# A gate's sums of squares by column blocks, and two token tiles to a PSUM bank

## The chip, the cores and the metric

The program runs on one core of a Trainium2 chip. The time is the device time of one execution in microseconds (us); a kernel's time is the median of its runs. The profile comes from one more execution of the same program.

## What is computed

Two layers of an encoder trunk on 512 tokens of 1024 values, all in float32. Each layer has mixers (three groups of heads), a layer of 16 experts that each take 64 tokens, and at its end an embedding that is let in through a gate. The change is in this last part:

```
x = x + expert_choice_ffn(rmsnorm(x, g_ffn), ...)          # 16 experts; the last two matter here
e = rmsnorm(p[i] @ w_ple, g_ple)                           # computed earlier
gate = sigmoid(rmsnorm(x, g_ple_gate) @ w_ple_gate)        # [512, 1024] @ [1024, 1024]
x = x + e * gate
```

where `rmsnorm(x, g) = x * rsqrt(mean(x * x) + eps) * g`, the mean over a token's 1024 values.

## The kernel before

The 512 tokens are four token tiles of 128 (index t), the 1024 columns four column blocks of 256 (index c) or eight row blocks of 128 (index k) where they are contracted. A product in full float32 quality is made of three single-pass matmuls (`mm3`, lines 340 to 342): both operands are kept as a high and a low part, and the product of the two low parts is left out.

The function `moe` ends as follows. The last two experts' down projection goes by column blocks. For each c, TensorE multiplies with weights `wd` (line 1385) into `pY`; ScalarE and VectorE split the result into `yh` and `yl` (lines 1387, 1388); TensorE scatters them to the tokens, one product pair per token tile (lines 1392, 1393, PSUM tile `ysc`); VectorE adds that to x (line 1395). With that the columns of block c of x are final. TensorE then transposes them (line 1400, `nt`), and ScalarE and VectorE split the transposed block into `gTh` and `gTl` (the helper `split`, lines 269 and 271): the left operand of the gate's product, two row blocks k for each c. The norm is not applied to this operand: its gain g_ple_gate goes with the weights' rows, and its factor is applied when the product is read.

After the four blocks come four squares on ScalarE, one for each token tile, over all 1024 columns, each with an accumulated sum (line 1410). From the four sums VectorE makes the norm's factor `rg` by the helper `rsqrt`: four preparing steps (lines 175 to 178) and three Newton steps of three instructions (180 to 182), all on [128, 4], and a halving (1413).

Then the gate's products. For each column block c of the weights, and each token tile t, TensorE runs 8 x 3 matmuls into a PSUM tile `pgp` of [128, 256] (lines 340 to 342); ScalarE takes the tanh with `rg` as its scale (line 1425), VectorE does two steps with the embedding (1426) and x (1428), and in the last layer SyncE stores the block (1430). In layer 0 all of x is stored to a scratch (1434), for the next layer to read.

The PSUM tiles `pgp` and `pY` come from a pool of four buffers of one bank (2 KB per partition) each (`pg`). A buffer is given again when all who used it are done: for `pgp`, when the tanh has read it. The [128, 256] tile takes one such buffer and half of its bytes.

The gate's weights are loaded by SyncE's queue in four column blocks, multiplied by the gain on GpSimd (line 329), and split into `whi` on ScalarE (330) and `wlo` on GpSimd (332), each in four pieces of two row blocks. These and other large arrays take turns in 12 slots of 8 KB.

Semaphores and the order of the instructions on each engine are made by a planner, which simulates the program with its own costs and lets an engine take what is ready first, in the order of the text where several are. So gate products of block 0 stand between the last down projections in TensorE's order. The order on each engine is then fixed.

Of the kernel before, what the change touches and what calls it, by code (L numbers as in the profile page):

```python
# [15 lines left out]
ALU = mybir.AluOpType  # L16
# [20 lines left out]
# the tensor engine's waits in a step of the scan, in us  # L37
OWED = 0.5
# the pieces that go ahead of the scan
INIT = 3  # L40
FILLS = (1.9, 1.5, 1.1)
# the convolved columns' blocks of 128 (q 0-2, k 3-5, v 6-8) by column tiles, and w_out's tiles for groups A and B
# [4 lines left out]
def shape_constants():  # L47
    """Arrays that depend on the shapes alone, in one [128, n] block."""
# [36 lines left out]
    # log of the number of patterns that join two tokens, by partition and column offset  # L85
# [10 lines left out]
# per-layer small parameters by partition: [128, DEPTH, n]  # L96
PP = {"conv": (0, 45), "b_s": (45, 4), "qk_g": (49, 2), "g_ffn": (51, 8), "g_pg": (59, 8)}
PPW = 67
# per-layer row parameters, the same for every partition: [DEPTH, n]
# [5 lines left out]
def rr_(ap):  # L105
    """the same bytes, as operands of the single-pass product"""
    return ap.bitcast(F32R)


class K:  # L110
# [25 lines left out]
    def slot(self, name):  # L136
        """one of the 8 KB buffers that weights and passing activations share"""
        return self.cp.tile([128, 2048], F32, tag="slot", name=name, bufs=SLOTS)

    def gslot(self, name):  # L140
        """the same, for the scan's own arrays"""
        return self.cp.tile([128, 2048], F32, tag="gslot", name=name, bufs=2)

    def half(self, name):
        """half of such a buffer"""
        if self.halves is None:
            tv = self.slot(name)
            self.halves = tv[:, 1024:]
            r = tv[:, 0:1024]
        else:  # L150
            r, self.halves = self.halves, None
        return r.rearrange("p (k n) -> p k n", k=4)
# [16 lines left out]
    # ---- small helpers  # L169
    def rsqrt(self, y, ss, n, scale, eps):  # L170
        """y = (ss * scale + eps) ** -0.5 by three Newton steps; y, ss [128, n]; returns ss * scale + eps"""
# [13 lines left out]
    def rsqrt1(self, y, ss, scale, eps):  # L185
        """the same for one column"""
# [11 lines left out]
    # ---- start  # L198
# [12 lines left out]
    def setup2(self, l):  # L211
        """what only the mixers need"""
        nc, A = self.nc, self.A
        if l == 0:
            nc.scalar.dma_start(self.pp, A["pp"])
        self.mconst = self.one([128, CROUTE - CKEEP], "mcst")
        nc.scalar.dma_start(self.mconst, A["cst"][:, CKEEP:CROUTE])
        self.amask = self.one([128, S + 384], "amask")
# [39 lines left out]
    # ---- RMS norm of one token tile, with its gain  # L258
# [8 lines left out]
    def split(self, hi, lo, src, scale=1.0):  # L267
        """src (in PSUM) * scale as the sum of two parts that the single-pass product carries exactly"""
# [6 lines left out]
    def norm_T(self, t, h, hi, lo):  # L275
        """h [128 tokens, D] transposed into columns t of hi and lo, each a pair of [128, 4, S]"""
# [8 lines left out]
    # ---- weights  # L285
    def wtile(self, src, cols, nk=KD):
        """src [nk*128, cols] dram view, rows k*128+p -> [128, nk, cols]"""
# [4 lines left out]
    def wplan(self, specs):  # L292
        """(src, cols, nk) of the pairs that wnext will hand out, in their order"""
# [3 lines left out]
    def wload(self, small=False):  # L297
        """starts the load of the next weights, into one buffer or four small ones"""
# [12 lines left out]
    def wnext(self, ahead=True, small=False, gain=None, pieces=1, dve=0):  # L311
        """the next weights, times a gain by rows, as two parts that the single-pass product carries exactly"""
# [24 lines left out]
    def mm3(self, p, lh, ll, rh, rl, first, last):  # L337
        """p += (lh + ll).T @ (rh + rl) without the product of the two small parts"""
# [5 lines left out]
    def proj_tok(self, w, t, name):  # L344
        """token tile t of xn times the column tiles w"""
# [9 lines left out]
    def proj_cols(self, p, w, t, ks, k0=0):  # L355
        """the rows ks of one of these products, w from row k0"""
# [5 lines left out]
    # ---- one layer's mixers  # L362
    def mixer(self, l):
        nc, tc, A = self.nc, self.tc, self.A
        with tc.tile_pool(name=f"mix{l}", bufs=1, reuse_waits="tile") as mp:
# [5 lines left out]
            # in the order in which they end  # L371
# [32 lines left out]
            # the chunks' matrices wait for q and k alone  # L404
# [13 lines left out]
            # the scan's steps, and between them what does not wait for it  # L418
# [8 lines left out]
    def in_order(self):  # L427
        """a function that traces a generator's next piece, for the tensor engine after the pieces before it"""
# [17 lines left out]
    def interleave(self, lead, fill):  # L446
        """traces lead, whose pieces end with the time that the tensor engine would then wait, and in these waits the
        pieces of fill, which end with the time that they take; the tensor engine keeps this order"""
# [14 lines left out]
    # ---- group B: q and k  # L463
    def attn_qk(self, l, wq):
# [3 lines left out]
        # by pairs of heads; a head's q lies in its half of the partitions, the rest is zero  # L468
# [7 lines left out]
        # gains: of the rotated channels in the tables of sines, of the others at the transposition  # L476
# [15 lines left out]
        def second(i, t, qk):  # L492
            """blocks of two heads: 0 to 2 of q, 3 to 5 of k"""
# [44 lines left out]
    # ---- group A: gMLP, up to its transposed output  # L538
# [68 lines left out]
    # ---- group B: scores, softmax, values; a unit is one head's token tile  # L607
# [54 lines left out]
    # ---- group C: gate, decay and beta  # L662
    def gate_decay(self, l):
# [29 lines left out]
        # softplus(z) = max(z, 0) + log1p(exp(-|z|)), log1p(u) = 2 artanh(u / (2 + u))  # L693
# [15 lines left out]
        # g by direction, tiles in the order of the scan's steps  # L709
# [31 lines left out]
    # ---- group C: convolution, silu, q k v  # L741
    def gdn_qkv(self, l):
# [9 lines left out]
        for blocks in QKV_BLOCKS:  # L752
            wts = ahead or self.wnext()
            for b in blocks:
# [21 lines left out]
                if part < 2:  # L776
                    # by chunk: [k | q] in even chunks, [q | k] in odd ones
# [32 lines left out]
    def qk_norms(self, pss, ktok):  # L810
        """norms of k and q (twice their size, so eps is taken four times)"""
# [20 lines left out]
    # ---- group C: chunk matrices  # L832
# [41 lines left out]
    # ---- group C: (I + A)^-1 in place, a partition's two rows of matrices by direction  # L874
# [31 lines left out]
    # ---- group C: scan, both directions in step  # L906
# [77 lines left out]
    # ---- group C: norm, gate, transpose  # L984
    def gdn_out(self, l):
# [7 lines left out]
        # o is rq / 8 times the sum; gate is twice silu  # L993
# [20 lines left out]
    # ---- output projection: groups A and B, then C  # L1014
# [34 lines left out]
    def moe(self, l):  # L1049
# [4 lines left out]
        # the weights' first buffers where the mixers' arrays end first  # L1054
# [9 lines left out]
        # the norm's gain goes with the rows of w_router, the norm itself with the logits  # L1064
# [13 lines left out]
        # the affinities of a token tile, in rows of 32 for the transposition  # L1078
# [25 lines left out]
        # x as two parts that the single-pass product carries exactly; the norm goes with the experts' slots  # L1104
# [5 lines left out]
        # the CAP largest of an expert's two halves of a row, in descending order  # L1110
# [7 lines left out]
        # the CAP-th largest of both: the smallest of the larger ones, one list against the other reversed  # L1118
# [8 lines left out]
        # a token's slot, from 1: first those above it, then its equals, in the order of tokens; 0 for the others  # L1127
# [21 lines left out]
        def ple_e():  # L1149
            """ple embedding, normed and halved"""  # L1150
# [27 lines left out]
        # ---------- experts, two at a time: slots of one in partitions 0-63, of the other in 64-127  # L1178
# [3 lines left out]
        def gather(qd):  # L1182
# [25 lines left out]
            for pi in (2 * qd, 2 * qd + 1):  # L1208
# [14 lines left out]
                # of a slot: the gate, half the norm's factor, and half its square  # L1223
# [8 lines left out]
        # the weights' buffers in the order in which they come free: first those that the first pair needs only later  # L1232
# [3 lines left out]
        def taken(n, back=False):  # L1236
            """others take n slots"""
# [5 lines left out]
        def etile(src):  # L1243
            """256 rows of an expert's weights, by 128"""
# [16 lines left out]
        def gemm(ws, lhs, pt):  # L1261
            """both experts' products, weights by quarters"""
# [35 lines left out]
        for pi in range(NE // 2):  # L1298
# [9 lines left out]
            if pi == 0:  # L1308
                # the first products as soon as their rows are there
# [23 lines left out]
            if pi == 5:  # L1333
                # nothing gathers from x any more: it joins the experts' sum
# [26 lines left out]
        # ---------- the last two experts' results by columns, and with them the ple gate's left operand: the norm's  # L1361
        # gain goes with the rows of the weights, the norm itself with the gate
# [5 lines left out]
        sq2 = ep.tile([128, NT], F32, name="sq2")  # L1368
# [3 lines left out]
        for c in range(4):  # L1372
# [17 lines left out]
            for t in range(NT):  # L1390
# [4 lines left out]
                v.tensor_tensor(xv, p, xv, op=ALU.add)  # L1395
            self.mark("ple_gate")
# [11 lines left out]
        for t in range(NT):  # L1408
            junk = ep.tile([128, D], F32, tag="hid", name="junk", bufs=1)
            act.activation(junk, self.x(t), AF.Square, accum_out=sq2[:, t:t + 1])  # L1410
        rg = ep.tile([128, NT], F32, name="rg")
        self.rsqrt(rg, sq2, NT, 1.0 / D, EPS)
# [3 lines left out]
        for c in range(4):  # L1416
            cs = slice(256 * c, 256 * c + 256)
            wh, wl = self.wnext(gain=gp, pieces=4) if c else wg
            for t in range(NT):
                p = self.pg([128, 256], "pgp")  # L1420
                ts = slice(t * 128, (t + 1) * 128)
                for k in range(KD):
                    self.mm3(p, rr_(th_[:, k, ts]), rr_(tl_[:, k, ts]), wh[:, k, :], wl[:, k, :], k == 0, k == KD - 1)
                th = ep.tile([128, 256], F32, tag="OT", name="th5", bufs=3)
                act.activation(th, p, AF.Tanh, scale=rg[:, t:t + 1])  # L1425
                v.scalar_tensor_tensor(th, th, 1.0, e(t)[:, cs], op0=ALU.add, op1=ALU.mult)
                xv = self.x(t)[:, cs]
                v.tensor_tensor(xv, th, xv, op=ALU.add)
                if last or self.layers == 1:
                    nc.sync.dma_start(dst[:, t, cs], xv)  # L1430
# [20 lines left out]
def layout(inp):  # L1451
    """The launch's arrays: inputs as they are, or laid out anew."""
# [37 lines left out]
```

## Time and profile before

| | us |
|---|---|
| median of 3 runs | 1982.81 |
| lowest and highest run | 1973.91, 1988.45 |
| profiled execution, span from first to last instruction | 1976.9 |
| TensorE busy in it | 1804.5 (91%) |
| VectorE, ScalarE, GpSimd busy | 923.2, 517.4, 458.9 |

The page gives no time of the profiled execution beside its span. Times in the rows are counted from the start of the span; the end of layer 0's expert part and its gate lie at about 885 to 992 us, those of layer 1 at about 1865 to 1977 us. PE is TensorE, PEld its weight load, DVE is VectorE, ACT ScalarE, POOL GpSimd, SP SyncE. Several matmuls are under way at once, so the mean time of one (280 ns) is longer than the step from one to the next.

### The profile page before, as it was taken

Reading aid. Unit: us, or ns where it says so; the run is one execution under the profiler, and the core shown is the slowest. Engines: PE = TensorE matmul, PEld = TensorE weight load, DVE = VectorE, ACT = ScalarE, POOL = GpSimd, SP = SyncE. Lnnn points to the kernel's source line nnn. Section 1 sums busy time; section 2 is a strip of 40 time slices with the busy share of each in tenths; the row PEclk is TensorE's granted clock in tenths of the full one; section 3 lists DMA queues with packets and bytes.
Section 4 is the critical chain, followed back from the end, with each engine's and each line's share of the span. In section 5 each row is a group of like instructions: output and inputs, shape, how many; then the busy total and the mean of one; then the engine's idle time right before and its main releaser. Section 6 shows DMA issues by size and latency. Waiting matters only on the chain.

```text
span 1976.9 us, 29997 instructions
## 1 busy us (share of the span) xinstructions
PE 1804.5 (91%) x12216; PEld 1127.1 (57%) x12216; DVE 923.2 (47%) x2086; ACT 517.4 (26%) x1165; POOL 458.9 (23%) x402
## 2 busy tenths in 40 slices
PE   5898788979999999999889969899799999999997
PEld 5777666854434444335888757568435343443367
DVE  5879878651211211412587897776412221204134
ACT  4334444231101101102343344442211010011031
POOL 3544323410000003203445352232100000212042
PEclk9999889979999999999898979799799999999999
DMA  4212020388899999999242022005788999999971
GB/s 168 86 33 60 17 84 16 111 331 326 347 413 413 389 414 406 371 414 302 79 133 81 12 64 82 17 17 192 310 348 344 413 373 409 415 363 400 414 249 43
DMA packets 168729, 467.45 MB, mean 236 GB/s; under 512 B 11664, under 2 KB 68496, under 8 KB 168592
## 3 DMA queue, kind: packets, MB, share of 16 engines
q1 hardware_dynamic: 161504, 458.46, 60.3%
q10 hardware_dynamic: 7088, 7.09, 1.1%
q8 instruction: 96, 1.57, 0.3%
q14 instruction: 41, 0.34, 0.1%
HBM read 461.32 MB, written 4.19 MB: 235 GB/s over the span
## 4 chain that ended last, share of the span: by engine, by line
PE 67%; DVE 21%; ACT 4%; issue 3%; POOL 2%; DMA 2%; SPq 1%; ACTq 0%; DVEq 0%; POOLq 0%
PE pGt L1270 14%; PE pUp L1270 11%; PE pY L1270 10%; DVE acc L770 3%; PE xep L1198 2%; DVE rr L936 2%; PE ysc L1289 2%; PE xep L1199 2%; PE pgp L340 2%; PE op L340 1%; PE ysc L1290 1%; PE pgp L342 1%; PE pgp L341 1%; PE plep L1164 1%; PE pY L1385 1%
## 5 line engine op out<-in xcount | busy, mean ns | idle before, releaser
L1270 PE MATMUL pUp<-w,xe 128*64 128x512 f32 x800 | 200.8, 595 | 0.0
L1270 PE MATMUL pGt<-w,xe 128*64 128x512 f32 x640 | 200.4, 600 | 0.0
L332 POOL TENSOR_TENSOR wlo<-w,whi 128x512 fp32r<-128x512 f32 (+5 forms) x66 | 161.2, 2459 | 126.7 <-ACT whi L330 98.6
L1270 PE MATMUL pY<-w,hidT 128*64 128x512 f32 x720 | 190.0, 599 | 0.0
L1337 POOL TENSOR_TENSOR x<-x,hh 128x1024 f32<-128x1024 f32 x8 | 18.9, 2358 | 619.9 <-DVE x L1295 619.9
L1270 PEld LDWEIGHTS pUp<-w,xe 128*64 128x64 f32 x800 | 71.0, 137 | 101.5 <-issue 98.0
L1295 DVE TENSOR_TENSOR x<-ysc,x 128x512 f32<-128x512 f32 x96 | 63.2, 686 | 118.3 <-PE ysc L1290 118.3
L1270 PEld LDWEIGHTS pY<-w,hidT 128*64 128x64 f32 x720 | 65.2, 137 | 91.3 <-issue 88.7
L1270 PE MATMUL pGt<-wx,xe 128*64 128x512 f32 x320 | 115.2, 608 | 0.3
L1270 PEld LDWEIGHTS pGt<-w,xe 128*64 128x64 f32 x640 | 58.5, 136 | 99.8 <-issue 97.8
L1354 DVE SCALAR_TENSOR_TENSOR yl<-pY,gsl,yh 128x512 fp32r<-128x512 f32 x28 | 21.0, 751 | 166.8 <-ACT yh L1353 165.2
L1328 DVE SCALAR_TENSOR_TENSOR hid<-sg,gsl,pUp 128x512 f32<-128x512 f32 x32 | 23.7, 746 | 159.7 <-PE pUp L1270 158.2
L340 PE MATMUL pgp<-whi,gTh 128*128 128x256 f32 x256 | 74.8, 295 | 16.6 <-ACT th L1425 15.4
L1321 DVE SCALAR_TENSOR_TENSOR sg<-sg,pGt 128x512 f32<-128x512 f32 x32 | 21.8, 686 | 132.2 <-ACT sg L1320 132.2
L330 ACT ACTIVATE whi<-w 128x512 fp32r<-128x512 f32 (+5 forms) x66 | 67.3, 1057 | 38.9 <-PE op L341 15.4
L329 POOL TENSOR_TENSOR w<-w,pp 128x512 f32<-128x512 f32 x32 | 32.3, 1041 | 179.9 <-DMA wd<-in_w_e_down_dram 144.5
L341 PE MATMUL pgp<-wlo,gTh 128*128 128x256 f32 x256 | 73.4, 289 | 0.0
L342 PE MATMUL pgp<-whi,gTl 128*128 128x256 f32 x256 | 72.7, 293 | 0.0
L1320 ACT ACTIVATE sg<-pGt,gsl 128x512 f32<-128x512 f32 x32 | 21.8, 687 | 192.6 <-PE pGt L1270 190.6
L1200 ACT ACTIVATE xe<-xep,pp 128x256 f32<-128x256 f32 x64 | 30.2, 474 | 159.5 <-PE xep L1199 159.5
L1198 PE MATMUL xep<-OH,hh 128*128 128x256 f32 x256 | 69.1, 304 | 2.5 <-DVE OH L1186 2.5
L770 DVE SCALAR_TENSOR_TENSOR acc<-raw,pp,acc 128x512 f32<-128x512 f32 x72 | 64.1, 891 | 15.1 <-ACT acc L768 12.6
(403 smaller groups left out, 4214.5 us busy)
## 6 DMA issues: line engine op xcount, KB each, us to landing
w<-in_w_e_up_dram SPq DMA_DIRECT2D x100, 1024.0 KB, 14.3
w<-in_w_e_down_dram SPq DMA_DIRECT2D x90, 1024.0 KB, 11.6
w<-in_w_e_gate_dram SPq DMA_DIRECT2D x80, 1024.0 KB, 12.8
wx<-in_w_e_gate_dram SPq DMA_DIRECT2D x40, 1024.0 KB, 11.7
wx<-in_w_e_up_dram SPq DMA_DIRECT2D x28, 1024.0 KB, 12.1
wx<-in_w_e_down_dram SPq DMA_DIRECT2D x22, 1024.0 KB, 8.5
wd<-in_w_e_down_dram SPq DMA_DIRECT2D x32, 512.0 KB, 8.9
w<-in_w_in_dram SPq DMA_DIRECT2D x14, 1024.0 KB, 4.9
```

What stands on the lines that cost most here:

```text
L330: self.nc.scalar.activation(rr_(hi[:, ks, :]), wk, AF.Copy)
L332: e.tensor_tensor(rr_(lo[:, ks, :]), wk, hi[:, ks, :], op=ALU.subtract)
L340: pe.matmul(p, lh, rh, start=first, stop=False)
L341: pe.matmul(p, lh, rl, start=False, stop=False)
L342: pe.matmul(p, ll, rh, start=False, stop=last)
L770: v.scalar_tensor_tensor(acc, raw[:, kk:kk + S], conv[:, b, kk:kk + 1], acc, op0=ALU.mult, op1=ALU.add)
L936: v.tensor_tensor(rr[kl[dr], :], vtok[kl[dr], tl, :], fl(tm[kl[dr]]), op=ALU.subtract)
L1198: pe.matmul(p, rr_(hh[:, t, ks]), OHf[:, t, :], start=(t == 0), stop=False)
L1199: pe.matmul(p, rr_(hl[:, t, ks]), OHf[:, t, :], start=False, stop=(t == NT - 1))
L1270: pe.matmul(pt[nh][64 * ei:64 * ei + 64, :], lhs[:, kk, 64 * ei:64 * ei + 64], wt[ei][k][:, nh * 512:nh * 512 + 512], start=(kk == 0), sto ...
L1289: pe.matmul(p, rr_(OT[:, t, :]), rr_(yh[:, ns]), start=True, stop=False)
L1295: v.tensor_tensor(xv, p, xv, op=ALU.add)
```

## The change

First, the squares are taken by column blocks: after line 1395, as soon as a block of a token tile is final, ScalarE takes the square of that [128, 256] and its sum goes to a column of `sq2`, now [128, 4, 4]. After the blocks VectorE adds the four columns of each token tile, and `rsqrt` takes these sums. Second, the gate's products of the blocks 0 and 1 put two token tiles into one PSUM tile of [128, 2, 256], a whole bank: both tiles' matmuls come first, then both tanh. Blocks 2 and 3 keep one token tile to a buffer. The rest of the diff takes comments away.

```
-        sq2 = ep.tile([128, NT], F32, name="sq2")
+        sq2 = ep.tile([128, NT, 4], F32, name="sq2")
...
                 v.tensor_tensor(xv, p, xv, op=ALU.add)
+                junk = ep.tile([128, 256], F32, tag="hid", name="junk", bufs=1)
+                act.activation(junk, xv, AF.Square, accum_out=sq2[:, t, c:c + 1])
...
-        for t in range(NT):
-            junk = ep.tile([128, D], F32, tag="hid", name="junk", bufs=1)
-            act.activation(junk, self.x(t), AF.Square, accum_out=sq2[:, t:t + 1])
+        ssum = ep.tile([128, NT], F32, name="ssum")
+        v.tensor_reduce(ssum, sq2, axis=AX.X, op=ALU.add)
         rg = ep.tile([128, NT], F32, name="rg")
-        self.rsqrt(rg, sq2, NT, 1.0 / D, EPS)
+        self.rsqrt(rg, ssum, NT, 1.0 / D, EPS)
...
-            for t in range(NT):
-                p = self.pg([128, 256], "pgp")
-                ts = slice(t * 128, (t + 1) * 128)
-                for k in range(KD):
-                    self.mm3(p, rr_(th_[:, k, ts]), rr_(tl_[:, k, ts]), wh[:, k, :], wl[:, k, :], k == 0, k == KD - 1)
-                th = ep.tile([128, 256], F32, tag="OT", name="th5", bufs=3)
-                act.activation(th, p, AF.Tanh, scale=rg[:, t:t + 1])
+            n = 2 if c < 2 else 1
+            for t0 in range(0, NT, n):
+                p = self.pg([128, n, 256], "pgp")
+                for t in range(t0, t0 + n):
+                    ts = slice(t * 128, (t + 1) * 128)
+                    for k in range(KD):
+                        self.mm3(p[:, t - t0, :], rr_(th_[:, k, ts]), rr_(tl_[:, k, ts]), wh[:, k, :], wl[:, k, :],
+                                 k == 0, k == KD - 1)
+                for t in range(t0, t0 + n):
+                    th = ep.tile([128, 256], F32, tag="OT", name="th5", bufs=3)
+                    act.activation(th, p[:, t - t0, :], AF.Tanh, scale=rg[:, t:t + 1])
...
```

## Rows read from the trace of the kernel before

**Rows 1.** The page's chain of waits, shares of the span by engine
```profile
PE 67%; DVE 21%; ACT 4%; issue 3%; POOL 2%; DMA 2%; SPq 1%; ACTq 0%; DVEq 0%; POOLq 0%
```

**Rows 2.** Busy time by stretches, end of layer 0; columns in the first line
```profile
core 0: us, PE busy (x) PEld busy (x) DVE busy (x) ACT busy (x) POOL busy (x), PEclk, DMA share, GB/s
924.90:943.40 18.50, 17.92 (x142) 15.00 (x141) 7.06 (x19) 9.99 (x19) 13.04 (x12) 1.00 0.51 168
...
946.60:954.20 7.60, 0.00 (x0) 0.00 (x0) 6.75 (x8) 0.51 (x2) 6.77 (x7) 0.72 0.43 138
954.20:960.15 5.95, 5.93 (x28) 5.93 (x29) 2.89 (x8) 1.57 (x5) 0.00 (x0) 0.50 0.00 1
960.15:991.20 31.05, 31.05 (x263) 31.05 (x263) 17.00 (x39) 11.00 (x20) 10.98 (x9) 1.00 0.19 69
```

**Rows 3.** The same, end of layer 1
```profile
1928.50:1936.20 7.70, 0.01 (x1) 0.01 (x1) 6.82 (x8) 0.54 (x2) 6.84 (x7) 0.80 0.00 0
1936.20:1940.00 3.80, 3.80 (x18) 3.80 (x19) 2.89 (x8) 1.14 (x3) 0.00 (x0) 0.52 0.31 104
```

**Rows 4.** Instructions in order, TensorE: start, us, what, in brackets idle before, releaser
```profile
954.22 0.58 PE L340 MATMUL pgp<-whi,gTh 128*128 128x256 f32 x1 [7.71 <-ACT th L1425]
...
1936.19 0.58 PE L340 MATMUL pgp<-whi,gTh 128*128 128x256 f32 x1 [7.70 <-ACT th L1425]
```

**Rows 5.** Instructions in order, VectorE, layer 0, from the last block of x
```profile
940.06 0.42 DVE L1395 TENSOR_TENSOR x<-ysc,x 128x256 f32<-128x256 f32 x1 [0.69 <-PE ysc L1393]
942.33 0.49 DVE L175 TENSOR_SCALAR nr<-sq 128x4 f32<-128x4 f32 x1 [1.84 <-ACT junk L1410]
...
944.04 0.69 DVE L271 TENSOR_TENSOR gTl<-nt,gTh 128x512 fp32r<-128x512 f32 x1
944.64 1.08 DVE L181 TENSOR_TENSOR nr<-nr 128x4 f32<-128x4 f32 x1
...
952.43 0.96 DVE L182 SCALAR_TENSOR_TENSOR rg<-nr,rg 128x4 f32<-128x4 f32 x1
```

**Rows 6.** Instructions in order, GpSimd, layer 0: weights of blocks 1 to 3
```profile
933.75 5.04 POOL L332 TENSOR_TENSOR wlo<-w,whi 128x512 fp32r<-128x512 f32 x4
938.75 4.04 POOL L329 TENSOR_TENSOR w<-w,pp 128x512 f32<-128x512 f32 x4
944.42 4.96 POOL L332 TENSOR_TENSOR wlo<-w,whi 128x512 fp32r<-128x512 f32 x4 [1.63 <-ACT whi L330]
949.34 4.03 POOL L329 TENSOR_TENSOR w<-w,pp 128x512 f32<-128x512 f32 x4
```

**Rows 7.** Instructions in order, ScalarE, layer 0: fourth square, first tanh
```profile
941.14 1.06 ACT L1410 ACTIVATE junk<-x 128x1024 f32<-128x1024 f32 x1
...
953.69 1.20 ACT L1425 ACTIVATE th<-pgp,rg 128x256 f32<-128x256 f32 x3 [7.79 <-DVE rg L1413]
```

**Rows 8.** Groups by line and form: count, busy us, mean ns, idle before
```profile
L1425 ACT ACTIVATE th<-pgp,rg 128x256 f32<-128x256 f32 x32 | 14.7, 473 | 64.0 <-PE pgp L342 47.2 <-DVE rg L1413 15.6 <-DVE x L1428 1.2
L1410 ACT ACTIVATION_READ_ACCUMULATOR junk<-x 128x1 f32 x8 | 1.5, 190 | 0.0
...
L561 DVE TENSOR_SCALAR mu<-mu 128x4 f32<-128x4 f32 x8 | 8.7, 1085 | 0.3
...
L1227 DVE TENSOR_REDUCE gsl<-pgs 128x1 f32<-128x2 f32 x16 | 2.6, 160 | 0.2
...
L176 DVE TENSOR_SCALAR nr<-nr 128x4 f32<-128x4 f32 x4 | 0.7, 170 | 0.1
```

**Rows 9.** Busy time by stretches, gate products (pgp) and their tanh alone
```profile
924.90:943.30 18.40, 10.80 (x72) 9.19 (x72) 0.00 (x0) 1.00 0.52 169
```

**Rows 10.** Instructions in order, GpSimd: last low weights of block 3, layers 0, 1
```profile
963.96 2.71 POOL L332 TENSOR_TENSOR wlo<-w,whi 128x512 fp32r<-128x512 f32 x2 [0.43 <-ACT whi L330]
...
1944.93 4.16 POOL L332 TENSOR_TENSOR wlo<-w,whi 128x512 fp32r<-128x512 f32 x3 [1.42 <-ACT whi L330]
```

**Rows 11.** Instructions in order, TensorE: first of layer 1, after the last gate product
```profile
991.17 1.04 PE L282 MATMUL nt<-cst,xs 128*128 128x128 f32 x8
```

**Rows 12.** Instructions in order, VectorE, layer 0: last step of block 0
```profile
956.77 0.42 DVE L1428 TENSOR_TENSOR x<-th,x 128x256 f32<-128x256 f32 x1
```

More of the change, by code (lines that the diff above doesn't have):

```diff
@@ L1418, in moe @@
             wh, wl = self.wnext(gain=gp, pieces=4) if c else wg
-            for t in range(NT):
-                p = self.pg([128, 256], "pgp")
-                ts = slice(t * 128, (t + 1) * 128)
-                for k in range(KD):
-                    self.mm3(p, rr_(th_[:, k, ts]), rr_(tl_[:, k, ts]), wh[:, k, :], wl[:, k, :], k == 0, k == KD - 1)
-                th = ep.tile([128, 256], F32, tag="OT", name="th5", bufs=3)
-                act.activation(th, p, AF.Tanh, scale=rg[:, t:t + 1])
[L1426 to L1430, printed above, removed]
+            n = 2 if c < 2 else 1
[9 more added lines that the diff above has]
+                    act.activation(th, p[:, t - t0, :], AF.Tanh, scale=rg[:, t:t + 1])
+                    v.scalar_tensor_tensor(th, th, 1.0, e(t)[:, cs], op0=ALU.add, op1=ALU.mult)
+                    xv = self.x(t)[:, cs]
+                    v.tensor_tensor(xv, th, xv, op=ALU.add)
+                    if last or self.layers == 1:
+                        nc.sync.dma_start(dst[:, t, cs], xv)
         if not last:
```

## The prediction

> **What bounds the kernel.** I read the page's chain of waits first: two thirds of the span is TensorE, most of the rest VectorE [rows 1]. So a change is worth what TensorE no longer waits. Then the busy time by stretches at the end of a layer, where the edited lines run. In layer 0 TensorE is busy while the last down projections and the first gate products alternate (924.9 to 943.4 us) and until 946.6, has nothing for 7.6 us, then runs 28 products in 5.95 us at a granted clock of 0.50 (the 1.2 GHz level), and only then 263 in 31.05 us at 1.00, the 2.4 GHz level [rows 2]. Layer 1 ends the same way [rows 3]. The order of instructions names the wait: the first product of column block 1 waits for a tanh of block 0, 7.71 and 7.70 us [rows 4]. All four PSUM buffers hold products of block 0, and their tanh needs the norm's factor rg.
>
> VectorE and ScalarE say why rg is late. x is final at 940.48 (its last block starts at 940.06). The fourth square, which queues behind three others, starts at 941.14, and the Newton chain opens at 942.33 [rows 5, 7]. The chain's [128,4] steps then take about 1 us each, from 944.64 to 953.4, while GpSimd runs weight work from 944.4 to 953.4 [rows 5, 6]; a small step of the same shape is 0.17 us on an average line [rows 8]. So the wait is the chain's slowness plus four PSUM buffers; the squares' own delay is about a microsecond of it.
>
> **Squares by blocks.** Removed, per layer: four squares of 1.06 us with a 0.19 us accumulator read each, about 5.0 us of ScalarE [rows 7, 8]. Added: sixteen of [128,256]. No row has that square; the nearest is the tanh of this shape, 0.473 us, and with the read 0.66 us, so 10.6 us [rows 8]. ScalarE is busy 9.99 of 18.5 us in that stretch [rows 2], so they fit; the cost is one square standing in front of yh or of a transposed split, at most 0.66 us each time and seven times a layer (three yh, four pairs of splits), 4.6 us if nothing covers it. TensorE has the next block's down products and gate products for cover, so I take 0.3 us per layer and keep 4.6 as the end. Without that cover it would be all of it.
>
> The last square can start at 940.5 and end near 941.2, where the old one ended at 942.3: rg could come about 1.1 us earlier. The new sum over four columns on VectorE lies between 0.16 us (a reduction of two columns) and 1.09 us (a four-column step while GpSimd holds it up) [rows 8]; I take 0.3, the chain being partly clear of GpSimd there. Both matter only if rg is still waited for.
>
> **Shared banks.** Blocks 0 and 1 now take two buffers each, so TensorE may run all eight products of 24 matmuls before a tanh has to be done. The pace after the clock is back is 31.05/263 = 0.118 us a matmul [rows 2]. Block 0 ends at 946.5; block 1 would end 96 x 0.118 = 11.3 us later, at 957.8. Today's first three tanh start at 953.69 [rows 7], and VectorE finishes its two steps for all four tiles by 957.2 [rows 12]; block 2 needs one freed bank at 957.8 and the last one three products (8.5 us) later. So with rg no earlier than now there are 4 us of slack, and the wait goes whole. With it goes the slow clock: 28 matmuls would take 3.3 instead of 5.95 us, and in layer 1 18 would take 2.1 instead of 3.8 [rows 2, 3]. Gain: 7.7 + 2.6 in layer 0, 7.7 + 1.7 in layer 1, together 19.7 us.
>
> What is late next: the weights of block 3. Their low parts are ready at 966.7 and 1949.1 [rows 10]; TensorE would want them 192 matmuls (22.7 us) after block 0's end, at 969.2 and 1951.2, if GpSimd moves nothing. Margin 2.5 and 2.1 us; I count 0 and keep 2 us a layer as the end. Nothing swallows the gain at the layer's border: the next layer's first transposes follow the last product without a wait [rows 11], and the program's end is the same tanh, two VectorE steps and store. SyncE issues the same transfers in the same order; the next layer's weights wait for slots that come free earlier.
>
> **A bank in common has a price.** In the trace 72 of block 0's 96 products run before 943.3, between the last down projections [rows 9]: all four tiles are opened, six of eight row blocks each. If two tiles of one bank cannot both be open, only the first of each pair can run ahead: 36 products fewer, 36 x 0.118 = 4.2 us a layer moved behind the last split. Block 1's weights are ready at 938.8 [rows 6], in pieces from 935 on, and its first tiles have 36 such products to put in that place, if the planner does so. Between nothing and 4.2 us I take 0.8 us, nearer to nothing because TensorE has other work up to 930 and block 1's pieces are there from 935.
>
> The Trainium skill, PSUM — Partial Sum Buffer (The four PSUM rules), says that two accumulations open in one bank on the same partitions cannot both begin by clearing it: the later start makes the earlier sum be overwritten, so they have to run one after the other. By that rule, and with nothing in the gap, the sum would be 19.7 - 8.4 = 11.3 us; the trace of before has one tile to a bank here and cannot show it.
>
> **Sum.** 19.7 - 2 x (0.3 + 0.8) = 17.5 us. The profiled execution, 1976.9 us of span, would become 1959.4; the page gives no other time of it, and the median of the runs shown, 1982.8, lies 5.9 above. From the median: 1965.3 us. Runs of one kernel here lie 6 to 9 us from their median, so 1% (19.8 us) is about what tells a change from none.
>
> **Rivals.**
> - **The lead is lost (22%).** Tiles of one bank run in turn and block 1's products do not fill the gap. For it: 72 of 96 run ahead now. Against it: the weights are early enough. Gain 11.3 us: 1971.5.
> - **The chain takes the split's place (6%, slower).** VectorE runs in order. Today the last two low splits finish at 944.7, before the eight slow steps [rows 5]. With sums a microsecond earlier the planner can put the chain ahead of them; then the products of row blocks 6 and 7 wait for it, until about 953, and the clock drops again. From there 348 products are left (60 of block 0, 288 after it): 953 + 348 x 0.118 + 2.6 = 996.7 against 991.2 now, 5.5 us lost a layer: about 1994. It decides once the splits end after about 947.5 (991.2 - 41.1 - 2.6), that is, with three slow steps ahead of them. Against it: at 942.8 GpSimd pauses [rows 6], so steps moved forward run short.
> - **Nothing to show (13%).** Pairs free banks late, or block 3's weights and squares eat the gain: the wait moves to block 2 or 3 and 0 to 8 us are left, about 1979.
> - **The planner orders the rest of the kernel otherwise (4%)**: either side by 10 us or more; no row speaks to it.
>
> The forecast itself has 55%: its own range is 15 to 21 us (the top with the 0.58 us waits for the last split filled too), 1962 to 1968, and a few us for the runs' spread.
>
> **Numbers.** Predicted 1965.3. The range goes from full gain and a favourable spread, 1956, to the weak rival, 1979. Faster by over 1% means under 1963.0: the upper part of the forecast (somewhat over half of it, since its top and the runs' spread reach there), and half of the planner's case, 0.33. Within 1%: the rest of the forecast, the lost lead, the empty case and most of the chain's, 0.61. Slower by over 1% needs the chain's case in both layers and more, or the planner's, 0.06.
>
> **What would show it.** After: no wait of block 1's first product for a tanh; the clock at 1.00 through 946 to 960; the last gate product of layer 0 about 9 us nearer to the last down projection, and the same in layer 1. The lost lead: far fewer than 72 products in the stretch before the last split, with idle TensorE there. The chain's case: low splits of row blocks 6 and 7 after Newton steps on VectorE, and products waiting for them. I am wrong if a wait of several microseconds is left between blocks 0 and 2, or if layer 1's mixers change by more than these ends.

## The result and the profile after

The changed kernel takes 1959.88 us (median of 4 runs, 1958.17 to 1962.38), the kernel before on the same chip 1978.69 us (4 runs, 1973.91 to 1988.45): a ratio of 0.989, 95% interval 0.986 to 0.992. 1965.3 was predicted, with 1956 to 1979 as the range; the gain by these medians is 18.8 us against a forecast of 17.5. The ratio lies just at the 1% mark: the likelier of my three answers (within 1%) and the next one (faster by more) are not told apart by it.

The profiled execution took 1958.17 us, its span is 1956.2. So the spans differ by 20.7 us. The page's chain of waits barely changes against [rows 1]; one more point of TensorE in a shorter span is all it can say of a wait that went:

```profile
PE 68%; DVE 21%; ACT 4%; issue 3%; POOL 2%; DMA 2%; SPq 1%; ACTq 0%; DVEq 0%; POOLq 0%
```

The stretches of layer 0's end answer to [rows 2] (busy time of each engine by stretches, same columns as there):

```profile
core 0: us, PE busy (x) PEld busy (x) DVE busy (x) ACT busy (x) POOL busy (x), PEclk, DMA share, GB/s
940.00:945.24 5.24, 4.00 (x36) 3.79 (x33) 5.14 (x7) 3.39 (x6) 5.24 (x6) 1.00 0.60 203
945.24:947.40 2.16, 1.90 (x13) 1.70 (x14) 2.13 (x4) 0.00 (x0) 2.16 (x3) 0.98 0.00 0
947.40:950.70 3.30, 3.30 (x18) 3.30 (x17) 3.20 (x4) 0.00 (x0) 3.30 (x4) 0.50 0.39 101
950.70:983.90 33.20, 33.20 (x281) 33.20 (x281) 24.38 (x51) 12.85 (x24) 12.57 (x11) 1.00 0.24 86
```

The 7.6 us without TensorE work are gone. A granted clock of 0.50, the 1.2 GHz level, is still there: 18 matmuls in 3.30 us, 1.2 us more than at the later pace (33.20/281 = 0.118 us each). It comes earlier than before and behind another wait. The order of instructions on TensorE names it. These are all the gate products of both layers that wait, against [rows 4]; what released each is in brackets:

```profile
945.24 0.39 PE L342 MATMUL pgp<-whi,gTl 128*128 128x256 f32 x1 [1.25 <-DVE gTl L271]
946.47 0.39 PE L342 MATMUL pgp<-whi,gTl 128*128 128x256 f32 x1 [0.26 <-DVE gTl L271]
...
1913.41 0.58 PE L342 MATMUL pgp<-whi,gTl 128*128 128x256 f32 x1 [2.38 <-DVE gTl L271]
```

No product waits for a tanh any more. Three wait for the low part of a transposed block, which no product of before did. VectorE, in order, says why; this answers to [rows 5] (L271 is the low split, L1412 the new sum of four columns, L175 to L182 the Newton chain, L1415 the halving):

```profile
939.02 0.17 DVE L1412 TENSOR_REDUCE ssum<-sq 128x4 f32<-128x16 f32 x1 [0.88 <-ACT junk L1398]
939.22 0.17 DVE L175 TENSOR_SCALAR nr<-ssum 128x4 f32<-128x4 f32 x1
939.43 0.93 DVE L176 TENSOR_SCALAR nr<-nr 128x4 f32<-128x4 f32 x1
940.27 1.08 DVE L177 TENSOR_SCALAR nr<-nr 128x4 int32<-128x4 int32 x1
941.39 0.97 DVE L178 TENSOR_SCALAR rg<-nr 128x4 int32<-128x4 int32 x1
942.39 0.96 DVE L180 TENSOR_TENSOR nr<-rg 128x4 f32<-128x4 f32 x1
943.38 1.20 DVE L181 TENSOR_TENSOR nr<-nr 128x4 f32<-128x4 f32 x1
944.50 0.68 DVE L271 TENSOR_TENSOR gTl<-nt,gTh 128x512 fp32r<-128x512 f32 x1
945.10 0.71 DVE L182 SCALAR_TENSOR_TENSOR rg<-nr,rg 128x4 f32<-128x4 f32 x1
945.73 0.68 DVE L271 TENSOR_TENSOR gTl<-nt,gTh 128x512 fp32r<-128x512 f32 x1
...
952.32 0.17 DVE L1415 TENSOR_SCALAR rg<-rg 128x4 f32<-128x4 f32 x1
```

The sum and the first six steps of the chain stand ahead of the last two low splits, and five of the six are slow: 5.1 us. ScalarE had written the high parts by 941.24 (the first row below); so the splits could have started some 3 us before the first did. GpSimd shows what runs beside the slow steps, where [rows 6] had a pause of 1.63 us ahead of 944.42:

```profile
940.15 1.09 ACT L269 ACTIVATE gTh<-nt 128x512 fp32r<-128x512 f32 x2 [1.17 <-PE nt L1403]
```

```profile
935.55 3.79 POOL L332 TENSOR_TENSOR wlo<-w,whi 128x512 fp32r<-128x512 f32 x3
939.27 4.06 POOL L329 TENSOR_TENSOR w<-w,pp 128x512 f32<-128x512 f32 x4
943.27 5.00 POOL L332 TENSOR_TENSOR wlo<-w,whi 128x512 fp32r<-128x512 f32 x4
948.22 4.05 POOL L329 TENSOR_TENSOR w<-w,pp 128x512 f32<-128x512 f32 x4
```

It has no pause from 935.55 to 952.27, the whole length of the chain. Its pieces last 4.06/4 = 1.01 and 5.00/4 = 1.25 us, and a chain step beside them 0.93 to 1.08 and 1.20 us: one step to a piece.

For the comparison I use one length, the **gate stretch**: from the first of the last two experts' down products of a layer to its last gate product, on TensorE. In the profiled executions it is, in us:

| | layer 0 | layer 1 | waits of gate products in it (layer 0; layer 1) |
|---|---|---|---|
| before | 85.21 | 86.98 | gTh 0.58, tanh 7.71; 0.58, 7.70 |
| after | 77.24 | 79.11 | gTl 1.25 + 0.26; 2.38 |

So 7.97 + 7.87 = 15.8 of the 20.7 us come from the stretches that the change edits. Part of layer 1's share is not the change's: up to the first gate product TensorE runs the same products in both kernels, and that part takes 20.54 us before and 19.58 after (18.78 and 18.69 in layer 0). From the first gate product on, the stretches are 7.9 and 6.9 us shorter, together 14.8. The other 4.9 us lie outside the stretches, in lines that the change does not edit. Between the two stretches lie 894.3 us before and 888.9 after; 0.6 us of that is lost again ahead of the first one. There one of several differences is the wait for `qkTp` in layer 1's mixers, 10.9 us before and 9.2 after. I did not settle where the rest is; in the profiles below the part between the stretches takes 890.6 to 896.4 us, and the start of layer 0's stretch falls between 906.1 and 915.3 us over all of them.

### The profile page after: what moved, and what is told of

Read it like the earlier page. It is cut to its first block, busy times and chain, and to the rows that moved or that the text cites. A ratio compares the mean times of both kernels' runs of the same rounds, so it can differ in the third digit from the quotient of the medians.

```text
span 1956.2 us, 30065 instructions
## 1 busy us (share of the span) xinstructions
PE 1799.0 (92%) x12216; PEld 1126.8 (58%) x12216; DVE 930.7 (48%) x2088; ACT 523.6 (27%) x1213; POOL 457.6 (23%) x402
## 4 chain that ended last, share of the span: by engine, by line
PE 68%; DVE 21%; ACT 4%; issue 3%; POOL 2%; DMA 2%; SPq 1%; ACTq 0%; DVEq 0%; POOLq 0%
PE pGt L1270 15%; PE pUp L1270 11%; PE pY L1270 10%; DVE acc L770 3%; PE xep L1198 2%; DVE rr L936 2%; PE ysc L1289 2%; PE xep L1199 2%; PE op L340 1%; PE ysc L1290 1%; PE pV L943 1%; PE plep L1164 1%; PE pgp L342 1%; PE pgp L340 1%; PE pY L1385 1%
## 5 line engine op out<-in xcount | busy, mean ns | idle before, releaser
L330 ACT ACTIVATE whi<-w 128x512 fp32r<-128x512 f32 (+5 forms) x66 | 68.0, 1058 | 38.5 <-PE op L341 15.8
L1344 ACT ACTIVATE hidT<-htp 128x512 f32<-128x512 f32 x32 | 19.1, 597 | 193.5 <-PE htp L1343 193.5
```

The source lines that it names most:

```text
L330: self.nc.scalar.activation(rr_(hi[:, ks, :]), wk, AF.Copy)
```

## The experiments

My theory after this: the banks give the gain, by letting TensorE run on to block 2 without a tanh; the squares by blocks add nothing to it, and in this kernel they cost, because they bring the chain ahead of the last splits. The rivals: the squares do part of the work (the earlier chain shortens the wait), or the new wait is paid back elsewhere and costs nothing. Four kernels ran together with the kernel before (1989.23 us, 11 runs).

**The squares alone.** The changed kernel with one token tile to a bank in all blocks:

```
-            n = 2 if c < 2 else 1
+            n = 1
```

> The squares by blocks alone; every product has a PSUM buffer of its own again. Theory (the gain is the four more products that a bank for two tiles lets run before the first tanh): the wait for rg stays, so no gain, 0 to -1 us a layer; and since the whole Newton chain now stands ahead of the last two low splits on VectorE, the last 24 products of block 0 wait for it until about 952.5 us and the clock falls once: 953 + 312 x 0.118 + 2.6 = 992.4 against 991.2, about 1 us a layer lost, ratio to the kernel before 0.998 to 1.003. Rival (an earlier rg brings the gain): 4 us a layer or more, ratio 0.996 or less.

Measured: 1973.19 us, ratio 0.992 (0.990 to 0.994); stretches 78.48 and 79.98, with a wait for the tanh of 2.74 and 2.72 us where before had 7.7 (and 0.58 us for the last high part and 0.5 for a low one in each layer):

```profile
957.48 0.39 PE L340 MATMUL pgp<-whi,gTh 128*128 128x256 f32 x1 [2.74 <-ACT th L1432]
```

The squares alone give 6.7 and 7.0 us a layer, 6.9 and 5.3 from the first gate product on. That is the rival's side, and much more than the microsecond by which the sums come earlier. VectorE and, below it, GpSimd show the reason:

```profile
949.51 0.96 DVE L176 TENSOR_SCALAR nr<-nr 128x4 f32<-128x4 f32 x1
950.39 0.15 DVE L177 TENSOR_SCALAR nr<-nr 128x4 int32<-128x4 int32 x1
...
951.77 0.16 DVE L182 SCALAR_TENSOR_TENSOR rg<-nr,rg 128x4 f32<-128x4 f32 x1
951.85 0.68 DVE L271 TENSOR_TENSOR gTl<-nt,gTh 128x512 fp32r<-128x512 f32 x1
...
954.45 1.19 DVE L182 SCALAR_TENSOR_TENSOR rg<-nr,rg 128x4 f32<-128x4 f32 x1
```

```profile
946.40 4.05 POOL L329 TENSOR_TENSOR w<-w,pp 128x512 f32<-128x512 f32 x4
951.87 4.97 POOL L332 TENSOR_TENSOR wlo<-w,whi 128x512 fp32r<-128x512 f32 x4 [1.42 <-ACT whi L330]
```

GpSimd pauses from 950.45 to 951.87, waiting for ScalarE's high parts, and in that pause VectorE runs eight steps of 0.15 to 0.17 us. In the kernel before the pause was there too, but two splits of 0.69 us stood in it among four short steps, and eight steps of about 1 us came after it [rows 5, 6]. So what makes rg late is how many of the chain's steps meet GpSimd's work, and a somewhat earlier start can change that: rg is ready 8.9 us after x here and 13.1 us before. It is an accident of the order: the changed kernel has the same squares and no pause.

**The pairs alone.** The changed kernel with the squares as they were:

```
-        sq2 = ep.tile([128, NT, 4], F32, name="sq2")
+        sq2 = ep.tile([128, NT], F32, name="sq2")
...
-                junk = ep.tile([128, 256], F32, tag="hid", name="junk", bufs=1)
-                act.activation(junk, xv, AF.Square, accum_out=sq2[:, t, c:c + 1])
...
-        v.tensor_reduce(ssum, sq2, axis=AX.X, op=ALU.add)
+        for t in range(NT):
+            junk = ep.tile([128, D], F32, tag="hid", name="junk", bufs=1)
+            act.activation(junk, self.x(t), AF.Square, accum_out=sq2[:, t:t + 1])
```

> The shared banks alone; four whole squares after the blocks as before. On VectorE the last low splits now stand ahead of the whole chain. Theory: rg comes at about 953 to 954 us as before, and nobody waits for it, because eight products may run first; no wait for the low splits either. The whole 9 to 10 us a layer: ratio 0.988 to 0.991, at or a little below the changed kernel. Rival (the squares by blocks are needed for the gain): half of it or less, 0.994 or more.

Measured: 1953.99 us, ratio 0.984 (0.982 to 0.987); stretches 74.15 and 73.76, and no gate product waits in either. By the stretches, half of the change does better than the whole. VectorE has the two last splits ahead of the chain:

```profile
940.73 1.29 DVE L271 TENSOR_TENSOR gTl<-nt,gTh 128x512 fp32r<-128x512 f32 x2 [2.75 <-ACT gTh L269]
942.25 1.03 DVE L175 TENSOR_SCALAR nr<-sq 128x4 f32<-128x4 f32 x1 [0.24 <-ACT junk L1410]
```

**The splits first.** The changed kernel, with the sum, the chain and the halving told to be issued behind the last split:

```
                 self.split(th_[:, k, :], tl_[:, k, :], p)
+                end = nc.cur_bb.bb.instructions[-1]
...
+        with tc.issue_after(end):
             v.tensor_reduce(ssum, sq2, axis=AX.X, op=ALU.add)
             self.rsqrt(rg, ssum, NT, 1.0 / D, EPS)
             v.tensor_scalar(rg, rg, 0.5, None, op0=ALU.mult)
```

> The changed kernel, with the sum, the Newton chain and the halving put behind the last low split on VectorE. Theory (in the changed kernel the chain's slow steps stand ahead of the splits and cost 1.5 and 2.4 us of waiting, with a spell at 1.2 GHz after it): the waits for gTl go, the clock stays at 1.00, rg comes at about 953 us and nobody waits for it: 3 us a layer better than the changed kernel, ratio to before 0.985 to 0.987. Rival (the waits are only shifted: rg comes later and block 2 waits for it): the same as the changed kernel, 0.989, with a wait for a tanh in its place.

Measured: 1956.32 us, ratio 0.984 (0.982 to 0.986); stretches 73.81 and 73.83, no gate product waits, and the granted clock is 1.00 from the first gate product to the last in both layers. In layer 0 (the first stretch starts ahead of the last splits, the second ends 4 us short of the last product):

```profile
949.00:961.90 12.90, 12.90 (x112) 12.90 (x110) 11.85 (x17) 3.27 (x7) 11.95 (x11) 1.00 0.52 164
961.90:985.00 23.10, 23.10 (x197) 23.10 (x196) 19.73 (x34) 11.06 (x22) 11.29 (x9) 1.00 0.20 70
```

Against the changed kernel the order alone is worth 77.24 - 73.81 = 3.4 us in layer 0 and 79.11 - 73.83 = 5.3 us in layer 1, where 0.7 of it is in waits of the down products for their weights (1.6 and 0.9 us), so 4.6. With the splits in front, new squares and old squares give the same stretch to 0.3 us. So here the squares by blocks are worth nothing beside the pairs. The wait's price is more than its 1.5 and 2.4 us: the 1.2 GHz level that follows it costs 1.2 and 1.3 us more by the pace of 0.118 us a matmul. The remaining 0.7 and 0.9 us I cannot place.

**One block paired.** The changed kernel with pairs in block 0 alone, so that six products, not eight, fit before a tanh:

```
-            n = 2 if c < 2 else 1
+            n = 2 if c < 1 else 1
```

> The changed kernel, but only block 0 has two tiles to a bank: six products instead of eight can run before a tanh. Theory: TensorE runs dry 5.7 us earlier than with eight, at about 951 us in layer 0, and rg with its tanh is there at 953: a wait of 1 to 3 us a layer comes back with the slow clock after it, 3 to 5 us a layer worse than the changed kernel, ratio 0.992 to 0.995. Rival (six are as good as eight): 0.989.

Measured: 1967.05 us, ratio 0.990 (0.988 to 0.991); stretches 79.21 and 78.42. No gate product waits for a tanh; the low split is waited for 2.38 + 0.24 us in layer 0 and 2.32 in layer 1. That is the rival's side: in the changed kernel six products are enough, and the second pair is worth nothing in it. That is partly because its own wait for the split holds TensorE back while the chain goes on: it takes out of one wait what it puts into the other.

The other four ran together with the kernel before on another chip (1985.73 us, 11 runs). They were to tell whether the chain's slowness is the whole of the wait for the tanh, whether six products are still enough when the splits come first, and whether the best version holds.

**The chain in the clear.** The kernel before, neither part of the change in it. The gain that GpSimd multiplies into the weights of blocks 2 and 3 comes from a copy that is issued after the halving, so GpSimd's work on these blocks starts only when rg is done:

```
         v.tensor_scalar(rg, rg, 0.5, None, op0=ALU.mult)
+        half = nc.cur_bb.bb.instructions[-1]
+        gp2 = ep.tile([128, KD], F32, name="gp2")
+        with tc.issue_after(half):
+            v.tensor_copy(gp2, gp)
...
-            wh, wl = self.wnext(gain=gp, pieces=4) if c else wg
+            wh, wl = self.wnext(gain=gp2 if c > 1 else gp, pieces=4) if c else wg
```

> The kernel before, with neither part of the change. The gain of the gate weights of blocks 2 and 3 is read from a copy that VectorE makes after rg, so GpSimd works on these two blocks only once the Newton chain is through. Theory (the wait for rg is the overlap of the chain with GpSimd's weight work): the eight slow steps take 0.2 instead of 1 us each, rg is there at about 946.5 us as block 0's products end, the wait of 7.7 us shrinks to under 1 and the slow clock does not come: 8 to 10 us a layer, ratio 0.989 to 0.992. Rival (the four PSUM buffers alone hold TensorE, the chain is slow by itself): ratio 0.997 or more, the wait still 6 us or more.

Measured: 1966.32 us, ratio 0.991 (0.988 to 0.993); stretches 75.37 and 76.94. The waits for the tanh are 0.50 and 0.52 us, with the old squares and four single banks. TensorE, VectorE and GpSimd in layer 0:

```profile
954.21 0.39 PE L340 MATMUL pgp<-whi,gTh 128*128 128x256 f32 x1 [0.50 <-ACT th L1429]
```

```profile
951.85 0.15 DVE L181 TENSOR_TENSOR nr<-nr 128x4 f32<-128x4 f32 x1
...
953.22 0.16 DVE L182 SCALAR_TENSOR_TENSOR rg<-nr,rg 128x4 f32<-128x4 f32 x1
...
953.50 0.16 DVE L1417 COPY gp<-pp 128x8 f32<-128x8 f32 x1
```

```profile
940.87 5.04 POOL L332 TENSOR_TENSOR wlo<-w,whi 128x512 fp32r<-128x512 f32 x4
953.79 4.58 POOL L329 TENSOR_TENSOR w<-w,gp 128x512 f32<-128x512 f32 x4 [7.88 <-PE pgp L342]
```

With GpSimd idle from 945.9 to 953.8 every step of the chain takes 0.15 to 0.17 us. That shows what makes the wait in the kernel before: not the squares, but a chain of 14 small steps beside GpSimd's weight work, which four buffers are too few to bridge. Either cure removes the wait: this one, or the pairs alone, with the chain as slow as ever. The edit that holds GpSimd's work back takes 9.8 and 10.0 us from the stretches, where the whole change takes 8.0 and 7.9; from the first gate product on it is 9.9 and 8.8 against 7.9 and 6.9. In the totals the two are level.

**Six products with the splits first.** The third experiment with pairs in block 0 alone:

```
-            n = 2 if c < 2 else 1
+            n = 2 if c < 1 else 1
```

> The splits-first kernel, but only block 0 has two tiles to a bank. Theory: six products end about 1.7 us before the first tanh does there (960.6 against 962.3), so a wait of 1 to 2 us comes back in each layer, with the slow clock behind it: the gate's stretch 76 to 78 us instead of 73.8. Rival (six are as good as eight in any order): 73.8.

Measured: 1963.60 us, ratio 0.990 (0.988 to 0.993); stretches 76.57 and 76.47. TensorE waits again for a tanh:

```profile
960.61 0.39 PE L340 MATMUL pgp<-whi,gTh 128*128 128x256 f32 x1 [2.06 <-ACT th L1434]
```

and 2.29 us in layer 1. So when TensorE does not wait for the split, it comes to the seventh product about 2 us before rg's tanh, and the second pair, two products more, is what covers it: 76.5 against 73.8 us.

**The changed kernel again**, unedited, in the company of the next one:

> The changed kernel once more, beside the others. The gate's stretch 77 to 79 us again if its cost over the splits-first kernel is the order on VectorE, and its median 5 to 8 us above that kernel's, ratio to before 0.987 to 0.990; if the two are the same, the order costs nothing and the difference of the single profiles was chance.

Measured: 1967.42 us, ratio 0.992 (0.989 to 0.994); stretches 77.93 and 78.17, waits for the low split 2.38 us and 2.32 + 0.20. The same wait as in the first profile, in both layers. The ratio lies above the 0.987 to 0.990 that was expected; the splits-first kernel itself did not run in this company, the next one stands for it.

**All blocks paired, splits first.** The third experiment with `n = 2` in all four blocks:

```
-            n = 2 if c < 2 else 1
+            n = 2
```

> The splits-first kernel with two tiles to a bank in all four blocks. Theory: nothing waits for buffers any more, so blocks 2 and 3 gain nothing; at the end of each layer the last tanh of two tiles come together, 0.5 to 1.3 us more after the last product: ratio 0.984 to 0.986. Rival (tail sharing costs more, since x of two tiles ends late and the next layer's norm waits): 2 us or more a layer above the splits-first kernel.

Measured: 1960.13 us, ratio 0.988 (0.986 to 0.990); stretches 73.91 and 73.88, no waits. The ratio lies above the expected 0.984 to 0.986, the stretches within 0.1 us of the third experiment. So nothing is gained: with no wait left, pairs in blocks 2 and 3 have nothing to remove. At the very end they cost a little, as the last bank's two tanh come only after both products (layer 1's end on ScalarE and VectorE; the last product ended at 1953.7):

```profile
1953.71 0.84 ACT L1434 ACTIVATE th<-pgp,rg 128x256 f32<-128x256 f32 x2 [4.86 <-PE pgp L342]
1954.93 0.75 DVE L1437 TENSOR_TENSOR x<-th,x 128x256 f32<-128x256 f32 x2
```

x is final 2.0 us after the last product, and 1.4 us in the changed kernel. In this company the order of the splits, with the pairs in blocks 2 and 3, is worth 1967.4 - 1960.1 = 7.3 us, and by the stretches 4.0 and 4.3.

The best ratios are those of the pairs alone and of the splits first: 0.984, with intervals that end at 0.987 and 0.986, where the changed kernel's 0.989 has one from 0.986. So the totals alone hardly part them. The mended order is worth 0.005 of the time, some 10 us, by these ratios and 7.3 us in the second company, near the 7.5 us by which one kernel's median moves between two companies (the changed kernel: 1959.9 and 1967.4). The stretches, which repeat to a microsecond or so, carry the argument.

## Why the prediction was right, and where it was not

**What bounds the kernel: right.** The tanh of block 0 was the wait, and rg was its cause; both waits, 7.71 and 7.70 us, went in full, and the 0.58 us waits for the last high part with them. I also had the reason for rg's lateness right (slow steps beside GpSimd), and the experiment that clears the chain shows it.

**Squares by blocks: nearly free, as taken.** The new square costs less than its bound, 417 ns and 187 ns for the read against 473 and 190:

```profile
L1398 ACT ACTIVATE junk<-x x32: 399/417/420, 915.8 to 1905.5; 128x256 f32<-128x256 f32 x32
L1398 ACT ACTIVATION_READ_ACCUMULATOR junk<-x x32: 185/187/204, 916.2 to 1905.8; 128x1 f32 x32
```

(durations of the instructions of that line: least, median, most, in ns). No gate product or scatter waits for a `yh` or a high split behind one, so the 0.3 us a layer were not spent. The sum over four columns took 0.17 us, not 0.3. The halving starts at 952.32, 1.1 us sooner than at 953.42. That this is the number I had is luck: the chain began 3.3 us sooner, and from its first step to the halving it took 13.3 us where before it took 11.1.

**A bank in common: the rule holds, the price was nothing.** These are gate products and their tanh alone, against [rows 9]. Up to 945.20, in the 1.25 us wait that ends at 945.24, 77 products have run:

```profile
core 0: us, PE busy (x) PEld busy (x) ACT busy (x), PEclk, DMA share, GB/s
906.00:945.20 39.20, 11.15 (x77) 9.69 (x77) 0.00 (x0) 1.00 0.80 254
```

The first token tiles of four banks can have at most 80 by then: three for each of six row blocks, and two with the high part of row block 6, so 20 each. The second tiles had the same operands ready; yet TensorE goes idle at 77 rather than open them. The order behind the wait shows that they were unopened: each time a first tile's last product (line 342) is done, lines 340, 341 and 342 follow by turns for a whole tile of 24. So the program does not have two tiles of one bank open together. By the rule of the Trainium skill, PSUM — Partial Sum Buffer (The four PSUM rules), two accumulations open in one bank cannot both begin by clearing it, so tiles that each begin so have to run one after the other; the trace agrees, with its 77 products, the idle time and the unbroken tiles behind them. But block 1's first tiles were there to fill the place, as I had hoped, and TensorE ran 77 products ahead where it ran 72. With the splits first no gate product waits at all. "The lead is lost" did not happen.

**Block 3's weights: right.** The last low part is ready at 961.71 in layer 0 (5 us sooner than [rows 10]), and no product waits for it:

```profile
958.99 2.72 POOL L332 TENSOR_TENSOR wlo<-w,whi 128x512 fp32r<-128x512 f32 x2 [0.48 <-ACT whi L330]
```

**The chain takes the split's place: dismissed, and it came, at part of its price.** This is the step that failed. The rival set it at three slow steps ahead of the splits for a loss against before; five slow steps stood there. It did not turn the sign since the chain also began 3.3 us sooner (939.02 for 942.33): the splits end at 946.41, short of the 947.5 that I had worked out. What I put against it was that GpSimd pauses at 942.8, so that steps moved forward run short. That used a pause of the old order as if the new one had to keep it; after the change GpSimd works through from 935.55 to 952.27. The price is 3.4 and 4.6 us a layer against the kernel with splits first, of which 1.5 and 2.4 are the wait itself. At 6% the rival had far too little.

**The clock: half right.** The spell at 1.2 GHz behind the tanh wait went (2.6 and 1.7 us in my sum), but one behind the new wait gave 1.2 us of it back in layer 0, and about as much in layer 1 (10 matmuls in 2.20 us at 0.50, where 10 x 0.118 would be 1.2, and 35 in 4.40 at 0.87):

```profile
1913.40:1915.60 2.20, 2.19 (x10) 2.19 (x11) 2.17 (x4) 0.00 (x0) 2.20 (x3) 0.50 0.00 0
1915.60:1920.00 4.40, 4.40 (x35) 4.40 (x34) 3.84 (x6) 0.29 (x1) 3.59 (x4) 0.87 0.00 0
```

**The sum.** 17.5 us were expected from the two stretches and 15.8 came, one of these ahead of layer 1's first gate product and not by the change. So the sum from the gate products on is 14.8, not 17.5. Without the order's mishap even the 19.7 would have been too low: the kernel with splits first gains 11.4 us in each layer from the first gate product on, together 22.9. The 1.2 us of waits for the last high part explain a good third of the 3.2 us above 19.7. The total time came out close by luck: 4.9 us outside the stretches went the same way, and no term of mine stands for them. Of the 5.4 us between 1965.3 and 1959.9, 4.1 are the median of before, 1982.8 in three runs and 1978.7 in four.

**The signs.** Of those I had named, the wait for the tanh went. The clock did not stay at 1.00, the part between the stretches changed by more than my ends, and the last gate product came only 5.8 and 3.3 us nearer to the last down product, not 9: the last down product, too, comes sooner (it ends 6.7 us after the first gate product starts, where before it was 8.8 and 10.3 us).

**What stays open.** That the planner puts the chain ahead of the splits with new squares and behind them, or among them, with old ones was seen in the order and undone by an edit; why it does so no run here tells. Where the 4.9 us outside the stretches come from is told only in part.

## What to carry to other kernels

A long wait behind a chain of tiny steps can be shortened by more buffers (here 22 to 23 us in two layers), but look first for what slows the steps: holding one helper engine's work back until the chain was done won most of that, 18.6, without a buffer. When a change makes a chain ready sooner, ask what stands next to it on its in-order engine, and pin the order where the queue's neighbour feeds the busiest engine; a pause that the old order had is no cover in the new one. Do one part of a change alone before crediting both: here the half without the squares had the shorter stretches.

## What the runs showed of the hardware

VectorE's [128, 4] steps of the Newton chain take 0.15 to 0.17 us when GpSimd is idle. While it works on [128, 512] pieces most take 0.93 to 1.34 us, and 0.70 to 0.72 where a split stands between two steps; the first step (line 175) took anything from 0.17 to 1.09. The slow ones include steps with a single tensor operand and integer ones. The sum over four columns was not held up in any kernel: it takes 0.16 or 0.17 us beside GpSimd's work too, as at 939.02 in the changed kernel. In the kernel with splits first, both kinds stand in one chain; GpSimd's rows follow VectorE's:

```profile
951.07 0.93 DVE L176 TENSOR_SCALAR nr<-nr 128x4 f32<-128x4 f32 x1
951.92 1.33 DVE L177 TENSOR_SCALAR nr<-nr 128x4 int32<-128x4 int32 x1
...
960.01 0.96 DVE L182 SCALAR_TENSOR_TENSOR rg<-nr,rg 128x4 f32<-128x4 f32 x1
961.00 0.16 DVE L180 TENSOR_TENSOR nr<-rg 128x4 f32<-128x4 f32 x1
```

```profile
951.94 5.01 POOL L332 TENSOR_TENSOR wlo<-w,whi 128x512 fp32r<-128x512 f32 x4
956.91 4.04 POOL L329 TENSOR_TENSOR w<-w,pp 128x512 f32<-128x512 f32 x4
```

GpSimd's work ends at 960.95 and the next step is short. The Trainium skill, SBUF — State Buffer (SBUF: two separate sides), says that VectorE and GpSimd share a pair of ports that one of them holds for a whole instruction while the other is shut out, where VectorE's operation has two inputs in SBUF or runs in a mode of two ports. The trace agrees: a small step takes as long as GpSimd's piece of 1.01 or 1.25 us, however little it moves.

I had also not expected that a wait of 2.74 us can pass without a drop of the granted clock when one of 1.25 us is followed by one. In the kernel with the squares alone the stretch right behind its 2.74 us wait reads 1.00:

```profile
957.48:963.00 5.52, 5.52 (x46) 5.52 (x47) 5.43 (x8) 2.06 (x5) 3.90 (x4) 1.00 0.62 190
```

and in the changed kernel the stretch from 947.40, behind 1.25 and 0.26 us, reads 0.50. Nor does the wait's length decide within one kernel: in layer 1 of the kernel with the squares alone, the 2.17 us behind its wait of 2.72 us read 0.59. What makes the difference no run here tells.
